# Gated delta rule stage: dense tiles in another order, a pair's two heads half a step apart, own query norms per chain

## The chip, the cores and the metric

One core of a Trainium2 chip. The metric is the device time of one execution in microseconds (us); the core is alone, so its time is the kernel's time. TensorE's clock has two levels here, 1.2 and 2.4 GHz; the profile gives the granted clock as a share of the upper one (PEclk, 1.00 = always 2.4 GHz, 0.5 = always 1.2 GHz).

## The reference, cut to what matters

A decoder trunk over 512 positions and 1024 channels in float32: attention, a feed-forward layer, a gated delta rule layer (the stage that changes), a second feed-forward layer. The stage that changes computes:

```python
def gated_deltanet(u, w_in, conv_w, a_log, dt_bias, norm_gain, w_out):
    proj = u @ w_in                                   # 1024 -> q 1024, k 1024, v 2048, z 2048, b 16, a 16
    qkv = silu(causal_dwconv(proj[..., :QKV], conv_w))    # 4 taps over positions
    q = repeat(l2_norm(q) * 128 ** -0.5, 2)           # 8 q/k heads serve 16 v heads
    k = repeat(l2_norm(k), 2)
    o = chunk_gated_delta_rule(q, k, v, g(a), beta(b))
    o = rms_norm(o, norm_gain) * silu(z)
    return o.reshape(B, S, 2048) @ w_out

def step(state, inp):                                 # one chunk of positions, all heads
    v_new = u_c - w_c @ state
    o = qd_c @ state + qk_c @ v_new
    state = state * g_last + kd_c.T @ v_new
```

Inside a chunk u and w come from a unit lower-triangular system in k, beta and the decays.

## The kernel before

**Dense tiles.** Every projection is made of weight tiles of 128 x 1024. `weight` loads a tile (DMA issued by SyncE, `raw`, L136), ScalarE casts it to `whi` (L137), VectorE subtracts to get `wlo` (L138). `dense` then issues 24 matmuls of 128 x 512, three products (L148, L149, L150) for each of 8 k-steps, into one PSUM tile.

**The queue.** Everything that is not a dense tile is a generator. `pump` is called after every second k-step (6 dense matmuls, one unit of `now`) and runs the generators that are due; a generator yields the number of units until its next piece. So the program's order on each engine is written out when the program is built: pieces of generators stand between groups of dense matmuls, which cover their latencies on TensorE. Each engine works its list in order.

**The stage, about 594 to 1156 us of the profiled execution.** First the 8 k tiles. `post_qk` and `post_v` convolve a tile (`conv`: L563, three VectorE steps L565, L566), turn it by four TensorE transposes (`turn`, L573) and store it in DRAM (kt, vd). Then 23 to 24 tiles in the order "zzqzzqzzqzzqzzzzzzzzqqqq" (z: gates, stored as zd by L752; q: queries), then the 16 v tiles, then the output projection `gout` in 2 halves of 8 tiles each (a part of 6 k-steps, then the last 2 when their heads are done; the sum into the residual `hp` is L784).

Beside them run: decays of the 8 head pairs (TensorE L820 to L828, matrices D and kk); `solve`, which inverts the 32 x 32 diagonal blocks of all systems on VectorE in 30 steps of two instructions (L863 `tm<-X`, L865 `X<-X,tm`), yields after every second step, and stores the inverse X twice: as it is (Td, L869) and, through ScalarE copies L874, transposed (Nd, L875). `recur` then takes the 8 pairs one after the other. `prologue` of a pair loads kk, D, kt, qd, the blocks NT (L924) and TT (L928) and joins the blocks by small matmuls: L938, L949/L950, L961 (query times key), L969, L976, with VectorE's x (L942, L971), D (L963) and `qd` (L972, the queries times a decay row loaded from DRAM) between them and ScalarE's kd (L980). `chain` of a pair is the recurrence over 4 blocks of 128 positions, both heads in each step: L1001 (key times state S), L1003 (o), vb on VectorE (L1006), L1010 (solve times vb), vn on ScalarE (L1012), L1017 (state update), L1019 (o), squares of o (L1020), S (L1023 or L1027). `epilogue` makes the norm (`rsqrt`, L163 to L169), scales o (L1050), turns it, multiplies by the silu of z (L1054) and splits it for `gout`. The prologue of pair hk+1 is advanced step by step together with the chain of pair hk. All chains need `rq`, a norm over the squares of all 8 q tiles.

Of the kernel before, what the change touches and what calls it, by code (L numbers as in the profile page):

```python
# [17 lines left out]
P = 128  # L18
T = 512
NB = 4  # L20
# [6 lines left out]
def layout(x, positions, mixer_norm, ffn_norm, attn_w_in, attn_q_gain, attn_k_gain, attn_sinks,  # L27
# [29 lines left out]
    a["gout"] = c(gdn_w_out[0].reshape(2, 8, P, KT, P).transpose(0, 3, 2, 1, 4)).reshape(2, KT, P, 1024)  # L57
# [13 lines left out]
class Builder:  # L71
# [598 lines left out]
    def gdn(self, h, hd, stack, after):  # L670
# [13 lines left out]
        self.ssk = ss["k"]  # L684

        def post_qk(nm, j, ps):
# [14 lines left out]
            if j == 7 and nm == "q":  # L701
                self.rq = self.inv_norm(ss["q"], "rq")
                V.tensor_scalar(self.rq, self.rq, float(P ** -0.5), None, op0=ALU.mult)
                ready.add("rq")

        def post_v(hh, ps):
# [8 lines left out]
            self.aux.dma_start(d["v"][hh // 2, :, hh % 2], four(vb))  # L715
# [26 lines left out]
        count = {"z": 0, "q": 0}  # L742
        for nm in "zzqzzqzzqzzqzzzzzzzzqqqq":
            j = count[nm]
            count[nm] += 1
            if nm == "q":
                self.spawn(post_qk("q", j, self.in_tile(j, un)))
            else:
# [3 lines left out]
                self.aux.dma_start(d["z"][j // 2, :, j % 2], four(z))  # L752
            enter()
        for hh in range(16):
            self.spawn(post_v(hh, self.in_tile(16 + hh, un)))
            enter()
# [3 lines left out]
        for half in range(2):  # L760
            have = lambda n: lambda: all(("o", hh) in ready for hh in range(8 * half, 8 * half + n))
            early = 2
            self.until(have(6))
            part = []
            for m in range(KT):
                if half == 0:
                    nc.sync.dma_start(hp[m], hd[m])
                hi, lo = self.weight(self.ins["gout"][half, m])
                ps = self.psum()
                for k in range(6):  # L770
                    s = slice(k * P, (k + 1) * P)
                    self.mm3(ps, (hi[:, s], lo[:, s]), outs[8 * half + k], k == 0, False)
                    if k % 2:
                        self.pump()
                part.append((m, ps, hi, lo))
                if m < early - 1:
                    continue
                self.until(have(8))
                for m, ps, hi, lo in part:
                    for k in (6, 7):  # L780
                        s = slice(k * P, (k + 1) * P)
                        self.mm3(ps, (hi[:, s], lo[:, s]), outs[8 * half + k], False, k == 7)
                    self.pump()
                    V.tensor_tensor(hp[m], hp[m], ps, op=ALU.add)  # L784
                    if half == 1:
                        after(m, hp[m])
                part = []
# [3 lines left out]
    def decays(self, sp, X, ready):  # L791
# [24 lines left out]
        for hk in range(8):  # L816
# [14 lines left out]
            self.aux.dma_start(d["D"][hk], D)  # L831
# [10 lines left out]
            yield 2  # L842
        ready.add("systems")

    def solve(self, sp, X, ready):
# [14 lines left out]
        for j in range(1, 31):  # L860
# [5 lines left out]
            if j % 2 == 0:  # L866
                yield 1
        nc.gpsimd.memset(X.rearrange("p i s c -> p i (s c)")[:, :, ::33], 1.0)
        self.aux.dma_start(d["T"].rearrange("m p i s c -> (m p) i s c"), X)  # L869
        for i in range(2):  # L870
            for b in range(2):
# [3 lines left out]
                self.aux.dma_start(d["N"].rearrange("m p i c s -> (m p) i c s")[:, i, cs], nat)  # L875
        ready.add("solved")

    def recur(self, rx, ready, outs):
        nxt = self.prologue(rx, 0, ready)
        w = yield from nxt  # L880
        for hk in range(8):
            cur = w
            chain = self.chain(rx, hk, cur, ready)
# [236 lines left out]
```

## Time and profile before

| | |
|---|---|
| time, median of 3 runs | 1555.14 us (1555.0 to 1555.92) |
| time of the profiled execution | 1552.91 us |
| its span | 1551.0 us |
| PE busy in the span | 1488.9 us, 96% |
| DVE / ACT / POOL busy | 890.0 / 686.7 / 10.4 us |
| mean granted clock | 0.982 |
| chains: first and last start of L1010 | 857.7 and 1109.9 us |

The span is what the trace shows; 1.9 us of the profiled execution lie outside of it, and it was 2.2 us shorter than the median run. PE is TensorE, PEld its weight load, DVE VectorE, ACT ScalarE, POOL GpSimd, SPq SyncE's instructions that issue DMAs. An engine's idle time is put down to what released it.

### The profile page before, as it was taken

The page shows a single profiled execution, that of the slowest core. Times are in us where ns is not written, and L with a number is a line of the kernel's source. Part 1 is how long each engine was busy: PE and PEld are TensorE (multiplying, and loading weights), DVE is VectorE, ACT ScalarE, POOL GpSimd, SP SyncE. Part 2 cuts the span into 40 slices and gives each one's busy share as a digit, 9 for nine tenths or more (in the row PEclk, how much of TensorE's full clock was granted, in tenths as well). Part 3 has the DMA queues.
Part 4 walks back from the last instruction along what each step waited for, and adds up shares of the span by engine and source line. Part 5 has one row for each costly group of instructions (what it writes and reads, how often), then busy time and mean ns, then how long its engine had stood idle before and what let it go on. Part 6 is the DMA issues. An engine that isn't in the chain of part 4 may idle for free.

```text
span 1551.0 us, 21045 instructions
## 1 busy us (share of the span) xinstructions
PE 1488.9 (96%) x7962; PEld 1228.9 (79%) x7962; DVE 890.0 (57%) x1759; ACT 686.7 (44%) x1576; POOL 10.4 (1%) x21
## 2 busy tenths in 40 slices
PE   7998999999999999999969998999999999999998
PEld 7965788888888888788748777878788888888887
DVE  7575765446535557754846356655566535544652
ACT  6687643223313345665335455644543323332331
POOL 0000000000000000000000000000000000000000
PEclk9998999999999999999979998999999999999999
DMA  5201233223333233367663444453132333222232
GB/s 179 69 25 32 82 109 95 96 95 95 98 100 102 96 129 119 122 203 244 203 212 113 126 150 147 156 144 109 57 108 95 98 102 99 95 95 96 95 103 74
DMA packets 83084, 177.09 MB, mean 114 GB/s; under 512 B 31272, under 2 KB 35368, under 8 KB 82728
## 3 DMA queue, kind: packets, MB, share of 16 engines
q1 hardware_dynamic: 82984, 175.76, 35.7%
q8 instruction: 62, 1.02, 0.3%
q14 instruction: 38, 0.31, 0.1%
HBM read 149.42 MB, written 26.31 MB: 113 GB/s over the span
## 4 chain that ended last, share of the span: by engine, by line
PE 85%; DVE 5%; DMA 5%; ACT 4%; issue 1%; SPq 0%; POOL 0%; DVEq 0%
PE ps L148 25%; PE ps L149 25%; PE ps L150 25%; DMA qd<-rowd 3%; ACT sc L520 1%; PE ps L573 1%; DVE wlo L138 1%; PE ps L545 1%; PE ps L961 1%; PE ps L1010 1%; DVE sc L514 1%; PE ps L1017 1%; PE ps L1003 1%; PE ps L1019 1%; PE ps L511 1%
## 5 line engine op out<-in xcount | busy, mean ns | idle before, releaser
L148 PE MATMUL ps<-a,whi 128*128 128x512 f32 x1736 | 691.1, 398 | 3.5 <-ACT whi L137 2.3
L149 PE MATMUL ps<-a,whi 128*128 128x512 f32 x1736 | 680.4, 392 | 0.0
L150 PE MATMUL ps<-a,wlo 128*128 128x512 f32 x1736 | 680.0, 392 | 0.1
L137 ACT CAST whi<-raw 128x1024 fp32r<-128x1024 f32 (+1 forms) x239 | 242.5, 1015 | 474.1 <-PE ps L149 406.3
L148 PEld LDWEIGHTS ps<-a,whi 128*128 128x128 f32 x1736 | 327.2, 189 | 76.6 <-ACT a L143 3.4
L150 PEld LDWEIGHTS ps<-a,wlo 128*128 128x128 f32 x1736 | 327.1, 188 | 70.3 <-DVE wlo L138 0.3
L149 PEld LDWEIGHTS ps<-a,whi 128*128 128x128 f32 x1736 | 327.4, 189 | 65.8 <-DVE a L144 1.1
L138 DVE TENSOR_TENSOR wlo<-raw,whi 128x1024 fp32r<-128x1024 f32 (+1 forms) x239 | 280.7, 1175 | 96.5 <-ACT whi L137 94.1
L258 DVE TENSOR_TENSOR h<-h,ps 128x512 f32<-128x512 f32 x48 | 33.0, 688 | 148.5 <-PE ps L150 148.5
L243 DVE TENSOR_TENSOR t<-ps,rbc 128x512 f32<-128x512 f32 x48 | 33.2, 691 | 106.6 <-PE ps L150 106.4
L249 DVE TENSOR_TENSOR t<-ps,rbc 128x512 f32<-128x512 f32 x48 | 33.2, 692 | 90.8 <-PE ps L150 90.8
L247 ACT ACTIVATE t<-t 128x512 f32<-128x512 f32 x48 | 30.4, 632 | 97.4 <-DVE t L246 97.4
L148 PE MATMUL ps<-whi,a 128*128 128x256 f32 x192 | 57.3, 299 | 9.1 <-ACT a L192 9.1
L149 PE MATMUL ps<-wlo,a 128*128 128x256 f32 x192 | 55.6, 290 | 0.5 <-DVE wlo L138 0.5
L150 PE MATMUL ps<-whi,a 128*128 128x256 f32 x192 | 55.6, 290 | 0.0
L148 PEld LDWEIGHTS ps<-whi,a 128*128 128x128 f32 x192 | 38.0, 198 | 11.2 <-ACT a L192 9.1
L143 ACT CAST a<-t 128x512 fp32r<-128x512 f32 x48 | 30.0, 624 | 33.0 <-DVE t L250 33.0
L244 ACT ACTIVATE t<-t,cols 128x512 f32<-128x512 f32 x48 | 38.9, 811 | 2.0 <-DVE t L243 2.0
L565 DVE SCALAR_TENSOR_TENSOR t<-ps,cols,t 128x511 f32<-128x511 f32 (+2 forms) x48 | 35.8, 746 | 6.5 <-ACT t L563 6.0
L149 PEld LDWEIGHTS ps<-wlo,a 128*128 128x128 f32 x192 | 38.2, 199 | 0.7 <-DVE wlo L138 0.7
L150 PEld LDWEIGHTS ps<-whi,a 128*128 128x128 f32 x192 | 38.0, 198 | 0.1
L246 DVE SCALAR_TENSOR_TENSOR t<-t,cols,t 128x510 f32<-128x510 f32 x48 | 36.0, 750 | 1.7
(255 smaller groups left out, 1410.3 us busy)
## 6 DMA issues: line engine op xcount, KB each, us to landing
raw<-in_up SPq DMA_DIRECT2D x96, 512.0 KB, 3.7
raw<-in_down SPq DMA_DIRECT2D x48, 512.0 KB, 3.6
raw<-in_gin SPq DMA_DIRECT2D x48, 512.0 KB, 3.8
raw<-in_gout SPq DMA_DIRECT2D x16, 512.0 KB, 3.9
raw<-in_win SPq DMA_DIRECT2D x10, 512.0 KB, 3.9
raw<-in_wout SPq DMA_DIRECT2D x16, 256.0 KB, 2.6
zd<-t SPq DMA_DIRECT2D x16, 256.0 KB, 3.2
Dd<-D SPq DMA_DIRECT2D x8, 512.0 KB, 2.7
```

Of the source, the lines that this page charges most:

```text
L137: nc.scalar.copy(hi[:, s], raw[:, s])
L138: nc.vector.tensor_tensor(lo[:, s], raw[:, s], hi[:, s].bitcast(F32), op=ALU.subtract)
L148: mm(ps, w[0], x[0], start=first, stop=False)
L149: mm(ps, w[0], x[1], start=False, stop=False)
L150: mm(ps, w[1], x[0], start=False, stop=last)
L243: nc.vector.tensor_tensor(g, gu[0], self.bc, op=ALU.mult)
L244: nc.scalar.activation(y, g, AF.Identity, bias=self.col(C_FB + l * 24 + j), scale=self.col(cw + 2))
L246: nc.vector.scalar_tensor_tensor(y[:, 2:], g[:, :T - 2], self.col(cw), y[:, 2:], op0=ALU.mult, op1=ALU.add)
L247: nc.scalar.activation(y, y, AF.Silu)
L249: nc.vector.tensor_tensor(t, gu[1], self.bc, op=ALU.mult)
L258: nc.vector.tensor_tensor(h[m], h[m], ps, op=ALU.add)
L565: nc.vector.scalar_tensor_tensor(dst[:, i:], g[:, :T - i], self.col(cw + 3 - i), dst[:, i:], op0=ALU.mult, op1=ALU.add)
```

## The change

1. **Order.** After the k tiles: "zzqzzvzzvzzqzzvzzvzzzz", more tiles while `solve` runs, then "qvv" six times, each tile when the chains come to need it (`r < 3 * started`), between parts of `gout`, whose weights are laid out in 4 quarters of 4 tiles; a quarter runs when its four heads are done. A counter `live` bounds the buffers held.
2. **Grain.** The stage's tiles pump after every k-step, by half a unit (3 dense matmuls).
3. **Chains.** The two heads of a pair stand half a step apart, each with its own instructions (L1001's one 128 x 256 matmul becomes two of 128 x 128). The query norm `rq` is gone: the scale of q drops out of the final norm except in its EPS term, which `ep` now carries per head, so a chain needs its own pair's q tile only. `recur` starts the next pair's prologue as a process of its own.
4. **Prologue.** kd and qd are loaded first and multiplied on GpSimd (two ops each), NT and TT next, D and vb last; shorter yields; `solve` yields after every step.
5. **Stores** of kt, v, z, D and Nd are issued by ScalarE's queue, not SyncE's.
6. **Epilogue.** Squares as two 128 x 512 ACT ops and two DVE reductions per pair, in place of eight ACT ops with accumulation; one of the two heads is scaled on DVE.

```diff
-    def pump(self):
-        self.now += 1
+    def pump(self, w=1):
+        self.now += w
...
             if k % grain == grain - 1:
-                self.pump()
+                self.pump(grain / 2)
...
-        self.dense(ps, hi, lo, u)
+        self.dense(ps, hi, lo, u, grain=1)
...
-                self.aux.dma_start(d["kt"][j], t)
+                nc.scalar.dma_start(d["kt"][j], t)
...
-            if j == 7 and nm == "q":
-                self.rq = self.inv_norm(ss["q"], "rq")
...
-        for nm in "zzqzzqzzqzzqzzzzzzzzqqqq":
+        for nm in "zzqzzvzzvzzqzzvzzvzzzz":
+            tile_in(nm)
         self.until(lambda: "solved" in ready)
...
+        rest, r, g = "qvv" * 6, 0, 0
+        while r < len(rest) or g < 12:
+            q = g // 4
+            if r < len(rest) and (r < 3 * self.started or not have(4 * q + 4)):
+                tile_in(rest[r])
...
+            elif have(4 * q + 4):
...
+                W = self.weight(self.ins["gout"][q, g % 4])
+                for m in (g % 4 * 2, g % 4 * 2 + 1):
+                    ps = self.psum()
+                    part(ps, m, W, q, range(4))
+                    end(ps, m, q)
...
+        self.until(lambda: have(14))
+        begun = []
+        for m in range(4):
...
+            part(ps, m, W, 3, (0, 1))
+            begun.append((ps, W))
+        self.until(lambda: have(16))
...
-            self.aux.dma_start(d["D"][hk], D)
+            nc.scalar.dma_start(d["D"][hk], D)
...
-            if j % 2 == 0:
-                yield 1
+            yield 1
...
-                self.aux.dma_start(d["N"].rearrange("m p i c s -> (m p) i c s")[:, i, cs], nat)
+                nc.scalar.dma_start(d["N"].rearrange("m p i c s -> (m p) i c s")[:, i, cs], nat)
...
+        self.aux.dma_start(qd, self.rowd[1, 1:, hs].partition_broadcast(P))
+        for j in range(2):
+            self.aux.dma_start(kd[:, j], d["kt"][hk].rearrange("p (n c) -> p n c", n=NB)[:, :NB - 1])
         self.aux.dma_start(kk, d["kk"][:, hs])
-        self.aux.dma_start(D, d["D"][hk])
-        self.aux.dma_start(kt, d["kt"][hk].rearrange("p (n c) -> p n c", n=NB))
-        self.aux.dma_start(qd, self.rowd[1, 1:, hs].partition_broadcast(P))
...
-            yield 16
+            yield 4
...
-        yield 3
+        self.aux.dma_start(D, d["D"][hk])
+        if early:
+            self.aux.dma_start(vb, d["v"][hk])
+        yield 4 if hk else 8
+        for j in range(2):
+            ck = self.ck[:, :NB - 1, 2 * hk + j].unsqueeze(2).broadcast_to([P, NB - 1, P])
+            nc.gpsimd.tensor_tensor(kd[:, j], kd[:, j], ck, op=ALU.mult)
...
+        for j in range(2):
+            nc.gpsimd.tensor_tensor(qd[:, :, j], self.qT[hk][:, P:].rearrange("p (n c) -> p n c", c=P), qd[:, :, j], op=ALU.mult)
...
-        V.tensor_tensor(qd, self.qT[hk][:, P:].rearrange("p (n c) -> p n c", c=P).unsqueeze(2).broadcast_to([P, 3, 2, P]), qd, op=ALU.mult)
...
-                nc.tensor.matmul(pk[:, :2 * P], self.kT[hk][:, s], S.rearrange("p j c -> p (j c)"), start=True, stop=True)
...
+                    mm(pk[:, col(j)], self.kT[hk][:, s], S[:, j], start=True, stop=True)
+                    V.scalar_tensor_tensor(vb[:, j, n], pk[:, col(j)], at(self.ca, j), vb[:, j, n], op0=ALU.mult, op1=ALU.add)
+                    mm(o[j][:, s], qd[:, n - 1, j], S[:, j], start=True, stop=False)
+                    yield 1 if j else 0.5
...
+                mm(pv[:, col(j)], TT[:, j, n], vb[:, j, n], start=True, stop=True)
+                nc.scalar.copy(vn[:, j], pv[:, col(j)])
+                yield 0.5
...
+            nc.scalar.activation(ob[j], o[j], AF.Square)
+            V.tensor_reduce(mo[:, j], four(ob[j]), axis=AX.X, op=ALU.add)
```

SyncE's list at the end of the solve (X the inverse, Nd and Td its stores in DRAM, NT and TT their loads, zd the store of a z tile, raw a weight tile), before:

```order
L136 DMA raw<-in_gin 128x1024 x4
L875 DMA Nd<-t_6710 128x512
L869 DMA Td<-X 128x2048
L875 DMA Nd<-t_6713 128x512
L875 DMA Nd<-t_6716 128x512
L875 DMA Nd<-t_6719 128x512
L752 DMA zd<-t_6722 128x512
L752 DMA zd<-t_6756 128x512
L752 DMA zd<-t_6790 128x512
L752 DMA zd<-t_6824 128x512
L752 DMA zd<-t_6858 128x512
L924 DMA NT<-Nd 32x8x32 x3
```

The same place on SyncE after the change:

```order
L1063 DMA z<-zd 128x1024
L136 DMA raw<-in_gin 128x1024 x6
L898 DMA Td<-X 128x2048
L950 DMA NT<-Nd 32x8x32 x2
L954 DMA TT<-Td 32x8x32 x2
L950 DMA NT<-Nd 32x8x32
L954 DMA TT<-Td 32x8x32 x6
L958 DMA vb<-vd 128x1024
L136 DMA raw<-in_gin 128x1024
```

The stores of Nd and zd have left the list (ScalarE issues them now), and two TT loads stand between the NT loads.

VectorE's list inside the solve (each step is a pair L863, L865), before:

```order
L863 TENSOR_TENSOR tm<-X 128x468
L865 TENSOR_TENSOR X<-X,tm 128x2x13x18
L863 TENSOR_TENSOR tm<-X 128x476
L972 TENSOR_TENSOR qd<-a_6120,qd 128x768
L865 TENSOR_TENSOR X<-X,tm 128x2x14x17
L138 TENSOR_TENSOR wlo<-raw,whi 128x1024
```

The same place on VectorE after the change (L893 and L895 are the steps, t_6675 a v tile in its convolution):

```order
L138 TENSOR_TENSOR wlo<-raw,whi 128x1024
L895 TENSOR_TENSOR X<-X,tm 128x2x11x20
L565 SCALAR_TENSOR_TENSOR t_6675<-ps,cols,t_6675 128x511
L893 TENSOR_TENSOR tm<-X 128x456
L565 SCALAR_TENSOR_TENSOR t_6675<-ps,cols,t_6675 128x510
L895 TENSOR_TENSOR X<-X,tm 128x2x12x19
L565 SCALAR_TENSOR_TENSOR t_6675<-ps,cols,t_6675 128x509
L893 TENSOR_TENSOR tm<-X 128x468
L138 TENSOR_TENSOR wlo<-raw,whi 128x1024
```

`qd` no longer stands between two steps; convolutions of v tiles do, since v tiles are now made during the solve.

TensorE's list inside a chain step (L148 to L150 are dense matmuls of a tile), before:

```order
L1010 MATMUL ps<-vb,TT 128x128 x2
L148 MATMUL ps<-a_5192,whi 128x512
L149 MATMUL ps<-a_5193,whi 128x512
L150 MATMUL ps<-a_5192,wlo 128x512
L148 MATMUL ps<-a_5237,whi 128x512
L149 MATMUL ps<-a_5238,whi 128x512
L150 MATMUL ps<-a_5237,wlo 128x512
L1017 MATMUL ps<-vn,kd 128x128 x2
L1019 MATMUL ps<-vn,D 128x128 x2
```

The same step on TensorE after the change (L1043, L1049 and L1054 are the new numbers of L1010, L1017 and L1019):

```order
L1043 MATMUL ps<-vb,TT 128x128
L148 MATMUL ps<-a_9705,whi 128x512
L149 MATMUL ps<-a_9706,whi 128x512
L150 MATMUL ps<-a_9705,wlo 128x512
L1049 MATMUL ps<-vn,kd 128x128
L1054 MATMUL ps<-vn,D 128x128
L148 MATMUL ps<-a_9283,whi 128x512
L149 MATMUL ps<-a_9284,whi 128x512
L150 MATMUL ps<-a_9283,wlo 128x512
L1049 MATMUL ps<-vn,kd 128x128
L1054 MATMUL ps<-vn,D 128x128
```

The pair of each matmul is parted by three dense matmuls, the first head's L1043 standing three more ahead of this piece.

## Rows read from the trace of the kernel before

**Rows 1.** Stretches of the span: busy us of each engine, PEclk, DMA share, GB/s.

```profile
860.00:940.00 80.00, 72.24 (x632) 61.91 (x632) 44.00 (x106) 40.77 (x127) 2.52 (x4) 0.88 0.44 128
920.00:940.00 20.00, 14.85 (x147) 12.67 (x146) 11.42 (x33) 9.16 (x30) 0.96 (x1) 0.84 0.48 151
940.00:1000.00 60.00, 57.37 (x463) 49.13 (x463) 35.27 (x75) 34.17 (x101) 2.53 (x4) 0.97 0.48 146
1000.00:1060.00 60.00, 55.56 (x472) 47.44 (x471) 35.77 (x90) 31.95 (x101) 2.53 (x4) 1.00 0.51 154
1060.00:1090.00 30.00, 27.70 (x239) 23.37 (x238) 17.19 (x43) 13.04 (x39) 0.00 (x0) 0.94 0.34 102
1160.00:1551.00 391.00, 387.05 (x1711) 320.24 (x1710) 197.04 (x237) 120.46 (x142) 0.00 (x0) 1.00 0.29 95
```

**Rows 2.** TensorE's waits, 594 to 1160 us: in total, times, longest.

```profile
PE ps L938 <- DMA NT<-Nd: 14.4, 1, 14.4
PE ps L949 <- DVE nt L167: 5.1, 1, 5.1
PE ps L949 <- DVE x L942: 3.7, 4, 2.5
PE ps L1017 <- ACT vn L1012: 3.6, 3, 2.6
PE ps L949 <- issue: 3.2, 2, 2.2
PE ps L1010 <- DMA vb<-vd: 2.5, 1, 2.5
PE ps L148 <- ACT whi L137: 2.3, 1, 2.3
PE ps L573 <- ACT t L1050: 1.2, 1, 1.2
```

**Rows 3.** VectorE's waits, 640 to 1121 us.

```profile
DVE qd L972 <- DMA qd<-rowd: 28.6, 7, 6.9
```

**Rows 4.** SyncE's waits, 640 to 1121 us.

```profile
SPq L752 <- ACT t L751: 17.4, 10, 7.2
```

**Rows 5.** TensorE in time: start, us, instruction, idle before it and its releaser.

```profile
721.96 0.40 PE L828 MATMUL ps<-a,selr 128*128 128x512 f32 x1
...
795.03 0.31 PE L938 MATMUL ps<-NT,kk 32*32 32x32 f32 x2 [14.43 <-DMA NT<-Nd]
```

**Rows 6.** VectorE in time, start and end of the solve and one step.

```profile
736.71 2.35 DVE L858 TENSOR_TENSOR X<-X,bk 128x1024 f32<-128x1024 f32 x2
...
761.87 0.96 DVE L972 TENSOR_TENSOR qd<-a,qd 128x768 f32<-128x768 f32 x1 [2.37 <-DMA qd<-rowd]
...
784.77 0.26 DVE L865 TENSOR_TENSOR X<-X,tm 128x60 f32<-128x60 f32 x1
```

**Rows 7.** ScalarE in time, behind the solve.

```profile
785.30 3.00 ACT L874 COPY t<-X 128x512 f32<-128x512 f32 x3
```

**Rows 8.** SyncE in time, behind the solve.

```profile
786.40 2.27 SPq L875 DMA_DIRECT2D Nd<-t  x3
788.81 3.30 SPq L752 DMA_DIRECT2D zd<-t  x5
792.16 1.90 SPq L924 DMA_DIRECT2D NT<-Nd  x3
```

**Rows 9.** Groups, 594 to 1160 us: busy, mean ns, idle before and releasers.

```profile
L138 DVE TENSOR_TENSOR wlo<-raw,whi 128x1024 fp32r<-128x1024 f32 x64 | 78.3, 1223 | 63.6 <-ACT whi L137 61.2 <-PE ps L1017 2.3
...
L565 DVE SCALAR_TENSOR_TENSOR t<-ps,cols,t 128x511 f32<-128x511 f32 x16 | 12.0, 748 | 6.1 <-ACT t L563 6.0
...
L784 DVE TENSOR_TENSOR h<-h,ps 128x512 f32<-128x512 f32 x16 | 10.9, 684 | 14.3 <-PE ps L150 14.3
...
L911 POOL MEMSET TT<- 128x1024 f32 x8 | 7.7, 959 | 818.7 <-DMA Dd<-D 718.4 <-PE ps L1010 61.8 <-ACT z L1045 15.4
L972 DVE TENSOR_TENSOR qd<-a,qd 128x768 f32<-128x768 f32 x8 | 7.7, 958 | 28.6 <-DMA qd<-rowd 28.6
```

More of the change, by code (lines that the diff above doesn't have):

```diff
@@ L751, in gdn @@
                 nc.scalar.copy(z, ps)
-                self.aux.dma_start(d["z"][j // 2, :, j % 2], four(z))
+                nc.scalar.dma_start(d["z"][j // 2, :, j % 2], four(z))
             enter()
-        for hh in range(16):
-            self.spawn(post_v(hh, self.in_tile(16 + hh, un)))
-            enter()
+        for nm in "zzqzzvzzvzzqzzvzzvzzzz":
+            tile_in(nm)
         self.until(lambda: "solved" in ready)
@@ L759, in gdn @@
         hp = self.load_h(stack)
[L760 to L768, printed above, removed]
-                ps = self.psum()
[L770 to L787, printed above, removed]
@@ new lines, in gdn, with part, end @@
+        have = lambda n: all(("o", hh) in ready for hh in range(n))
+        def part(ps, m, W, q, ks):
+            hi, lo = W
+            for k in ks:
+                s = slice((m % 2 * 4 + k) * P, (m % 2 * 4 + k + 1) * P)
+                self.mm3(ps, (hi[:, s], lo[:, s]), outs[4 * q + k], k == 0, k == 3)
+                self.pump(0.5)
+        def end(ps, m, q):
+            V.tensor_tensor(hp[m], hp[m], ps, op=ALU.add)
+            if q == 3:
+                after(m, hp[m])
+        rest, r, g = "qvv" * 6, 0, 0
@@ new lines, in gdn @@
+        self.until(lambda: have(14))
+        begun = []
+        for m in range(4):
+            if m % 2 == 0:
+                W = self.weight(self.ins["gout"][3, m // 2])
+            ps = self.psum()
+            part(ps, m, W, 3, (0, 1))
+            begun.append((ps, W))
+        self.until(lambda: have(16))
+        for m in range(KT):
+            if m < 4:
+                ps, W = begun[m]
+                part(ps, m, W, 3, (2, 3))
+            else:
+                if m % 2 == 0:
+                    W = self.weight(self.ins["gout"][3, m // 2])
+                ps = self.psum()
+                part(ps, m, W, 3, range(4))
+            end(ps, m, 3)
@@ L977, in prologue @@
         nc.scalar.copy(TT[0:64, :, :, 64:128], view(pt[0:64, :], 64))
-        for j in range(2):
-            for n in range(3):
-                nc.scalar.activation(kd[:, j, n], kt[:, n], AF.Copy, scale=self.ck[:, n, 2 * hk + j:2 * hk + j + 1])
-        yield 1
-        while ("v", 2 * hk) not in ready or ("v", 2 * hk + 1) not in ready:
+        if not early:
+            while not have_v():
+                yield 0.5
+            self.aux.dma_start(vb, d["v"][hk])
+            yield 3
+        else:
@@ L983, in prologue, with chain @@
             yield 1
-        self.aux.dma_start(vb, d["v"][hk])
-        yield 2
-        return TT, D, vb, kd, qd
-    def chain(self, rx, hk, tiles, ready):
+        return TT, D, vb, kd, qd, mo
+    def chain(self, rx, hk, tiles):
         nc = self.nc
         V = nc.vector
-        TT, qk, vb, kd, qd = tiles
+        mm = nc.tensor.matmul
+        TT, qk, vb, kd, qd, mo = tiles
         S = rx.tile([P, 2, P], F32, tag="S", name="S", bufs=2)
         o = [self.psum() for _ in range(2)]
-        self.o = o
-        self.mo = self.small.tile([P, 2, NB], F32, tag="mo", name="mo")
-        self.ob = [self.t2() for _ in range(2)]
+        col = lambda j: slice(j * P, (j + 1) * P)
@@ L1021, in chain @@
-            if n < NB - 1:
-                if n == 0:
-                    nc.scalar.copy(S, pu[:, :2 * P].rearrange("p (j c) -> p j c", j=2))
-                else:
-                    for j in range(2):
-                        h = 2 * hk + j
-                        V.scalar_tensor_tensor(S[:, j], S[:, j], self.egl[:, n, h:h + 1], pu[:, j * P:(j + 1) * P], op0=ALU.mult, op1=ALU.add)
-            if n < NB - 1:
-                yield
-    def epilogue(self, rx, hk, tiles, ready, outs):
+                mm(pv[:, col(j)], TT[:, j, n], vb[:, j, n], start=True, stop=True)
@@ L1051, in epilogue @@
+        for n in range(NB):
+            s = slice(n * P, (n + 1) * P)
+            nc.scalar.activation(ob[1][:, s], o[1][:, s], AF.Copy, scale=rs[:, 1, n:n + 1])
         yield 2
+        while self.live + 4 > 36:
+            yield 0.5
+        self.live += 4
         for j in range(2):
```

131 lines of the change are left out of this document (69 added, 62 removed).

## The prediction

> **What bounds the kernel now.** I read the page first: TensorE is busy 96% of the span, so only its idle time and its clock can be won. In the second feed-forward layer, which the change leaves alone, 1711 matmuls take 387.05 us at a clock of 1.00 [rows 1], 0.226 us each; that is the price of a dense matmul below, and the rate that the stage lacks. The stretches then show where it is lost inside the changed stage: from 860 to 940 us TensorE works 72.24 of 80 us at a clock of 0.88, then 57.37 of 60 at 0.97, and 27.70 of 30 at 0.94 [rows 1]. The waits of TensorE, of the stage alone, name the culprits: one of 14.4 us for the NT blocks, 5.1, 3.7 and 3.2 us at L949 in a prologue, 3.6 for vn, 2.5 for vb, 2.3 for a weight cast, 1.2 at the last epilogue [rows 2]. Two rows on other engines explain some of these. VectorE stands in its list seven times, 28.6 us in all and up to 6.9 at once, at `qd` L972 for a load [rows 3]; whatever is behind it, `x` and the norm's steps L167 among it, comes late, and these are what L949 waits for. SyncE stands 17.4 us in ten waits at the stores of z tiles [rows 4], with weight loads behind it.
>
> **The NT wait, 14.4 us.** Two paths race. TensorE: the last decay matmul starts at 721.96, the first matmul on NT at 795.03 after 14.43 us idle [rows 5], so TensorE arrives at 780.6. Between them I count 240 dense matmuls in the order (54.3 us), the 2.3 us weight wait and two turns with small things in the 1.8 us that are left, 0.9 a turn. In the changed order 283 dense matmuls and four turns stand there: 64.0 + 3.6, no weight wait (below), so TensorE arrives at 722.2 + 67.6 = 789.8. The solve: it starts behind L858, at 736.71 + 2.35 = 739.06, and its last step ends at 785.03 [rows 6], 46.0 us. Two `qd` steps leave it, one with a wait of 2.37 + 0.96 [rows 6] and one of 0.96, 4.3 us; seven convolution steps of v tiles come in at 0.748 [rows 9], 5.2 us. It ends at 786.0. Behind it the copies took to 788.30 [rows 7], and NT's matmul came 6.7 us later. Of these, 0.5 was the wait behind the z stores of 3.30 us for five [rows 8], which leave. New on the path: ScalarE issues the Nd stores itself between its copies, 1.4 (two of them at 0.66, the price of a store on SyncE [rows 8]); a z copy of 0.6 in place of a 1.0 cast; two TT loads between the NT loads, 1.3 (1.90 us for three such loads [rows 8]). NT is there at 786.0 + 3.3 + 6.7 - 0.5 + 1.4 - 0.4 + 1.3 = 797.8, the wait is 8.0 us: a gain of **6.4**. The ends are no wait and 17 (rivals).
>
> **Weight wait, 2.3 us.** The cast's tile came late because its load was issued behind a z store that waited for its copy. With the stores gone from SyncE no load stands behind one: **+2.3**. The Trainium skill, page "DMA: Bandwidth & Descriptors", section "Issuing engines are not separate DMA queues", speaks against it: transfers from several engines end on the same DMA engines, and spreading the issue saves only issuing time. By that the 2.3 would stay and the sum be that much smaller. The row of SyncE's waits [rows 4] shows something else than issuing time, a queue that stands for another engine's result, which the page doesn't treat; I keep the gain.
>
> **Prologue waits, 5.1 + 3.7 + 3.2 = 12.0 us.** `qd` leaves VectorE for GpSimd, which waits for the load alone, and the load is issued first instead of fourth. Nothing else on VectorE waits for a load in the prologue. Late next would be GpSimd's own kd and qd: four ops per pair of 128 x 384. No row shows such an op; a memset of 128 x 1024 takes 0.959 there [rows 9], so 0.36 by elements and, with three streams in place of one, 1.1 as the upper bound; VectorE's `qd` gives 0.48 (0.958 for 768 [rows 9]). Four cost 1.4 to 4.4 us in a pair's 32 us (chains run some 255 us for eight pairs), and their first reader is the chain behind the prologue: no cost. I take **+12.0**; the lower end is that half stays, since the waits at L949 are also the sequence of small steps itself.
>
> **vb, 2.5 us.** v tiles are made before they are asked for in pairs 0 to 3 and by need after; vb is loaded when both are stored, with three units between load and use (18 dense matmuls, 4.1 us). **+2.5**, none at the lower end.
>
> **Hops in the chains, 3.6 us.** Before, six dense matmuls (1.36 us) stood between a step's matmul and its reader. Now three, the other head's matmul, and three more; but a copy or a product is for one head, half as wide. The three waits came of ScalarE being late, and it now issues some fifty stores as well, at up to 0.66 each [rows 8], but loses 48 scalings for kd and 48 squares. I take 2.2 left: **+1.4**, ends 0 and 3.6. More instructions on TensorE (48 of 128 x 256 become 96 of 128 x 128) cost the same columns; I take 0.
>
> **Other work.** VectorE gains sixteen more sums at 0.684 [rows 9], sixteen reductions priced alike (nearest row of 512 columns) and eight half scalings: some 28 us, less 7.7 for `qd`. It is busy 44 of 80 us in the chains' busiest stretch [rows 1], so this lies in gaps: nothing, if the waits above stay away; each late step on it that reaches a chain is what the second rival prices.
>
> **Tail.** In the last epilogue a square and two reductions of 512 columns stand in a row ahead of the norm, three times 0.68, where before only the last block's square did. The 1.2 us wait [rows 2] becomes 2.7: **-1.5**. Ends: none and three times this.
>
> **Clock.** From 860 to 1090 the share missing from full clock is 80 x 0.12 + 60 x 0.03 + 30 x 0.06 = 13.2 us; at 92% busy 12 us of work lost [rows 1]. The stretches below full clock are those with the waits in them. Without them I leave 2.5 (the prologue of the first pairs): **+9.5**; half of it at the lower end. The clock lost around the NT wait I leave as it is.
>
> **Sum.** 6.4 + 2.3 + 12.0 + 2.5 + 1.4 - 1.5 + 9.5 = 32.6. On the profiled execution, 1552.9: 1520.3. That run was 2.2 below the median, so 1522.5, **1522**.
>
> **Rivals.**
> *The NT wait goes altogether.* For it: arrival and data differ by 8.0 only, and each is a long sum; a shorter hop through DRAM, or more dense matmuls than the turns leave room for, would do. Another 8.0 and 2.5 of clock: 1512. Chance 0.13.
> *Waits in the chains only halve.* The prologue stays a series of small steps between TensorE, VectorE and ScalarE, its yields are shorter than before, and VectorE has 20 us more to do. Half of 12.0 + 2.5 stays, 7.2, and 3.5 of the clock: 1533. Chance 0.19.
> *GpSimd holds up VectorE.* Eight of its new ops stand in the order during the solve, ahead of the memset that the Nd copies wait for. If each stops VectorE for its 1.1 us, the solve ends 8.8 later, and the NT wait is 16.8: 1531. Nothing in the trace shows it either way, GpSimd is busy 2.5 of 80 us there [rows 1]. Chance 0.08. The Trainium skill, "GPSIMD Engine Reference", section "Engine selection", puts two-input elementwise work at about half VectorE's speed on GpSimd; by it an op would be an estimated 0.96, near my upper bound.
> *The stores' move does nothing*, and a wait like the 2.3 remains: 1525. Chance 0.06.
> *The other side: the clock.* Half-sized pieces make small matmuls of 128 x 128 a finer mix with dense ones over all the chains. The 255 us of chains lose 0.92 x 255 = 235 us times what is missing from full clock. Without the 23.1 us of idle time that the sum wins and the 12 that the clock costs now, the change breaks even at 35.1 / 235, a mean clock of 0.85 there. The worst stretch so far, 920 to 940, has 0.84 [rows 1]; were the clock down half of the time over all the chains, 0.75, 58.7 us are lost: 1555.1 - 35.1 + 58.7 = 1579. Against it: 1000 to 1060 holds 1.00 with the same kinds of matmuls [rows 1]. Chance 0.05.
> *Nothing comes of it* (one new wait of 30 us takes the place of these, such as a tile that comes late because the order by need holds it): 1555. Chance 0.04.
>
> **How the numbers follow.** The forecast has 0.45; two runs of this kernel differ by about 0.1%, so I call under 0.2% (3 us) no change. All cases but the last two are faster: 0.91; same 0.03; slower 0.06. The range takes the first rival with 4 us of its own, and reaches up to the second with 7: 1508 to 1540, with the two last cases and the ends of the others left out.
>
> **What would show it.** Right: VectorE has no wait for `qd`; SyncE none at the z stores; TensorE's wait for NT is between 5 and 10 us; L981, the place of L949, under 3 us in all; the clock from 860 to 1090 at 0.97 or more; the stage ends some 33 us earlier and the feed-forward layer behind it takes as long as before. Wrong: a wait of TensorE for GpSimd's kd or qd, for a weight tile, or a clock under 0.9 in the chains; the solve longer than 48 us.

## The result, and the profile after

The changed kernel takes 1512.22 us (median of 4 runs, 1511.24 to 1513.94), the kernel before in the same comparison 1555.07; the ratio is 0.974 with a 95% interval of 0.9717 to 0.9764. The forecast was 1522 in 1508 to 1540: right in direction and range, 10 us too high. The two profiled executions are 39.0 us apart (1552.91 and 1513.94), and the sum of the prediction, 32.6, is to be held against these; that leaves 6.4 us. The other 3.9 lie in which executions were profiled: 2.2 us below the median before, 1.7 above it after.

The head of the page of the changed kernel: TensorE is busy 9.9 us less, and idle 29 us less.

```profile
span 1512.1 us, 21017 instructions
PE 1479.0 (98%) x8010; PEld 1218.7 (81%) x8010; DVE 907.3 (60%) x1761; ACT 661.6 (44%) x1424; POOL 41.4 (3%) x53
```

TensorE's waits in the stage of the changed kernel (columns as in [rows 2]); L970, L1043 and L1036 are the new numbers of L938, L1010 and L1001, and L210 belongs to the norm behind the stage:

```profile
PE ps L970 <- DMA NT<-Nd: 5.7, 1, 5.7
PE ps L210 <- DVE rc L169: 3.9, 1, 3.9
PE ps L1043 <- ACT vn L1044: 1.9, 2, 1.1
PE ps L573 <- ACT t L566: 1.2, 1, 1.2
PE ps L1036 <- DVE vb L1037: 0.8, 2, 0.6
PE ps L573 <- DVE t L1076: 0.7, 1, 0.7
```

TensorE waits for nothing in the prologues behind NT any more: all that L949 stood for in [rows 2] is gone. The largest wait is still NT, at 5.7 in place of 14.4. One wait is new, 3.9 us at L210. Stretches of the changed kernel, to be held against [rows 1]:

```profile
787.00:800.00 13.00, 7.34 (x50) 4.83 (x49) 0.85 (x2) 6.91 (x12) 0.00 (x0) 0.74 0.95 293
860.00:940.00 80.00, 79.19 (x663) 67.06 (x662) 57.13 (x118) 40.21 (x108) 9.92 (x13) 1.00 0.52 149
1113.00:1124.00 11.00, 7.06 (x30) 5.82 (x29) 6.42 (x20) 2.44 (x3) 0.00 (x0) 0.69 0.41 133
1124.00:1512.00 388.00, 384.55 (x1697) 318.08 (x1695) 194.38 (x234) 118.34 (x139) 0.00 (x0) 1.00 0.29 94
```

In the chains TensorE works 79.19 of 80 us at a clock of 1.00, where it worked 72.24 at 0.88. Inside the stage and at the norm behind it the clock is down only around the two long waits that are left, NT (0.74) and L210 (0.69). The feed-forward layer behind runs as before.

### The profile page after: what moved, and what is told of

Its sections match the earlier page's. It is cut to its first block, busy times and chain, and to the rows that moved or that the text cites. A ratio compares the mean times of both kernels' runs of the same rounds, so it can differ in the third digit from the quotient of the medians.

```text
span 1512.1 us, 21017 instructions
## 1 busy us (share of the span) xinstructions
PE 1479.0 (98%) x8010; PEld 1218.7 (81%) x8010; DVE 907.3 (60%) x1761; ACT 661.6 (44%) x1424; POOL 41.4 (3%) x53
## 3 DMA queue, kind: packets, MB, share of 16 engines
q8 instruction: 63, 1.03, 0.3%
## 5 line engine op out<-in xcount | busy, mean ns | idle before, releaser
L148 PE MATMUL ps<-a,whi 128*128 128x512 f32 x1736 | 696.2, 401 | 0.7 <-ACT a L143 0.7
L150 PE MATMUL ps<-a,wlo 128*128 128x512 f32 x1736 | 679.1, 391 | 0.0
L148 PEld LDWEIGHTS ps<-a,whi 128*128 128x128 f32 x1736 | 326.7, 188 | 68.9 <-ACT a L143 3.6
L150 PEld LDWEIGHTS ps<-a,wlo 128*128 128x128 f32 x1736 | 326.0, 188 | 68.8
L148 PE MATMUL ps<-whi,a 128*128 128x256 f32 x192 | 57.2, 299 | 8.3 <-ACT a L192 8.3
L150 PE MATMUL ps<-whi,a 128*128 128x256 f32 x192 | 55.6, 290 | 0.0
L148 PEld LDWEIGHTS ps<-whi,a 128*128 128x128 f32 x192 | 38.0, 198 | 10.3 <-ACT a L192 8.3
L150 PEld LDWEIGHTS ps<-whi,a 128*128 128x128 f32 x192 | 37.9, 198 | 0.1
L565 DVE SCALAR_TENSOR_TENSOR t<-ps,cols,t 128x511 f32<-128x511 f32 (+2 forms) x48 | 35.6, 742 | 3.5 <-ACT t L563 3.3
```

Of the source, the lines that this page charges most:

```text
L148: mm(ps, w[0], x[0], start=first, stop=False)
L150: mm(ps, w[1], x[0], start=False, stop=last)
L565: nc.vector.scalar_tensor_tensor(dst[:, i:], g[:, :T - i], self.col(cw + 3 - i), dst[:, i:], op0=ALU.mult, op1=ALU.add)
```

## The experiments

Each ratio is to the kernel before on the same chip (its time was 1547 to 1559 us over all of these runs). The changed kernel's own is 0.974, 0.9717 to 0.9764. Where a ratio and a difference of medians disagree, the ratio counts, since each is to runs of the kernel before made beside it.

| run | what differs | median us | ratio, 95% interval |
|---|---|---|---|
| before_qd_dve_first | before, qd load written first | 1551.31 | 1.0002, 0.9988 to 1.0015 |
| before_qd_pool | before, qd on GpSimd, load written first | 1527.29 | 0.985, 0.983 to 0.9871 |
| before_act_stores | before, stores on ScalarE | 1549.57 | 0.9992, 0.9977 to 1.0007 |
| after_qd_dve_late | after, qd on VectorE behind x2, load late | 1525.48 | 0.9837, 0.982 to 0.9853 |
| after_qd_dve | after, qd on VectorE, load early | 1528.83 | 0.9839, 0.9826 to 0.9853 |
| after_sync_stores | after, stores on SyncE | 1515.77 | 0.9755, 0.9741 to 0.9769 |
| after_cover | after, 4 units more ahead of NT | 1513.11 | 0.9734, 0.9714 to 0.9754 |
| after_norm_late | after, 2 units more ahead of L210 | 1506.81 | 0.9698, 0.9685 to 0.9711 |
| after_pair_same | after, both heads at one step | 1515.25 | 0.9771, 0.9758 to 0.9784 |
| before_qd_pool_cover | before_qd_pool, 7 units more ahead of NT | 1520.55 | 0.9799, 0.9776 to 0.9823 |
| norm_cover_pc | late norm, cover, heads together; steps not shorter, see below | 1512.24 | 0.9752, 0.9739 to 0.9766 |
| norm_cover_hs | late norm, cover, shorter steps, half step | 1502.55 | 0.9701, 0.9682 to 0.9721 |

**Where qd is multiplied: four runs.** The theory: VectorE's list stands at `qd` for its load, and what is behind it is late for L949. Rivals: a prologue is late of itself, or the load comes late wherever it is written. VectorE, then TensorE, in time in the kernel before, at the longest of these waits:

```profile
928.71 0.96 DVE L972 TENSOR_TENSOR qd<-a,qd 128x768 f32<-128x768 f32 x1 [6.87 <-DMA qd<-rowd]
...
934.49 0.43 DVE L942 TENSOR_TENSOR x<-ps,nbk 32x256 f32<-32x256 f32 x1
```

```profile
935.17 0.26 PE L949 MATMUL ps<-TT,x 32*32 32x32 f32 x2 [5.15 <-DVE nt L167]
```

L949 reads the `x` that is ready at 934.92. What `x` is made from, the result of L938, was there at 927.6, while VectorE stood at `qd`.

before_qd_dve_first (one line moved, the load written first):

```diff
+        self.aux.dma_start(qd, self.rowd[1, 1:, hs].partition_broadcast(P))
         self.aux.dma_start(kk, d["kk"][:, hs])
...
-        self.aux.dma_start(qd, self.rowd[1, 1:, hs].partition_broadcast(P))
```

> The kernel before, with one line moved: a pair's qd load is issued first of its prologue's loads in place of fourth; the multiplication stays on VectorE at its old place. Theory A (the waits at L949 come of VectorE standing for the qd load, 28.6 us in 7 waits): VectorE's wait at qd shrinks to under 15 us, TensorE's waits at L949 from 12.0 to under 6, the time falls by 4 to 14 us to about 1541 to 1551. Rival B (a prologue is late of itself, as a series of small steps): L949 keeps its 10 to 12 us, the time moves by less than 3 us. Rival C (the load is late because its buffer comes free late, wherever it stands in SyncE's list): VectorE's wait at qd stays above 20 us, the time moves by less than 3 us.

Nothing moved: the ratio is 1.0002. VectorE in this run stands at `qd` 32.7 us in eight waits, and TensorE at L949 as before. SyncE in time in this run (L916 loads kt, L913 is the moved qd load):

```profile
921.13 0.42 SPq L916 DMA_DIRECT2D kt<-ktd  x1
921.81 0.37 SPq L913 DMA_DIRECT2D qd<-rowd  x1
```

VectorE in time in the same run:

```profile
930.33 0.96 DVE L972 TENSOR_TENSOR qd<-a,qd 128x768 f32<-128x768 f32 x1 [6.15 <-DMA qd<-rowd]
```

The load still stands behind kt in SyncE's list, as it did in the kernel before: written first, it was not issued first, since its buffer comes free only with the last L1003 of two pairs ago. VectorE has the data 8.5 us after the issue. This is what the run's rival C expected. So the run doesn't show what an early load would do; it shows that the place in the source does not make it early.

before_qd_pool (the load as there, and the product on GpSimd):

```diff
-        V.tensor_tensor(qd, self.qT[hk][:, P:].rearrange("p (n c) -> p n c", c=P).unsqueeze(2).broadcast_to([P, 3, 2, P]), qd, op=ALU.mult)
+        for j in range(2):
+            nc.gpsimd.tensor_tensor(qd[:, :, j], self.qT[hk][:, P:].rearrange("p (n c) -> p n c", c=P), qd[:, :, j], op=ALU.mult)
```

> The kernel before with qd multiplied on GpSimd (two ops of 128 x 384 per pair) and its load issued first. Theory A: no wait of VectorE for qd is left, L949 waits under 3 us in place of 12.0, the clock from 860 to 1090 rises to 0.96 or more; the time falls by 12 to 21 us to about 1534 to 1543. Rival B (series of small steps): L949 keeps 8 us or more, the time falls by less than 6 us. Rival C (GpSimd takes over the wait): TensorE waits for qd at L1003 instead, 5 us or more, the time falls by less than 6 us.

The ratio is 0.985, some 23 us, more than half of the whole change by one operation on another engine, and more than the 12 to 21 us expected. TensorE's waits in the stage in this run, its three longest:

```profile
PE ps L938 <- DMA NT<-Nd: 11.8, 1, 11.8
PE ps L949 <- DMA TT<-Td: 3.5, 4, 1.8
PE ps L1011 <- DMA vb<-vd: 2.8, 1, 2.8
```

One stretch of the same run:

```profile
860.00:940.00 80.00, 78.69 (x657) 67.49 (x656) 51.83 (x118) 47.81 (x148) 6.82 (x9) 1.00 0.54 155
```

TensorE's idle pieces over 0.3 us sum to 25.9 in place of 39.9, and the clock of this stretch is 1.00 in place of 0.88. The span is 25.5 us shorter: 14 us of these waits and, as in the prediction's count, 10 to 11 of clock. Of the waits 2.6 us are at NT, where the solve is 2.1 us shorter without its two `qd` steps. L949 still waits some 5 us in all, mainly for the loads of TT, where under 3 was expected. GpSimd's own wait:

```profile
POOL qd L973 <- DMA qd<-rowd: 49.9, 7, 13.4
```

GpSimd stands for the load longer than VectorE did, 49.9 us, and TensorE doesn't wait for it: its waits name neither L1004, the reader, nor GpSimd. The wait was moved to a list with nothing urgent behind it. That contradicts rival B (L949 keeps 8 us or more) and this run's rival C (TensorE waits for `qd` at its reader instead). What the runs don't separate is the product itself, 0.96 us each time, from the wait ahead of it, since both leave VectorE together; but it is the smaller part, 7.7 us in eight [rows 9] against 28.6 of waits, and a wait like the 5.15 us above is longer than it.

after_qd_dve_late (the reverse, in the changed kernel: load behind kd and kk, product behind x2, as before) and after_qd_dve (load early as in the change, one VectorE op at GpSimd's place):

```diff
-        for j in range(2):
-            nc.gpsimd.tensor_tensor(qd[:, :, j], self.qT[hk][:, P:].rearrange("p (n c) -> p n c", c=P), qd[:, :, j], op=ALU.mult)
+        V.tensor_tensor(qd, self.qT[hk][:, P:].rearrange("p (n c) -> p n c", c=P).unsqueeze(2).broadcast_to([P, NB - 1, 2, P]), qd, op=ALU.mult)
```

> The changed kernel with qd multiplied on VectorE behind x2 as before, and its load issued behind kd and kk. Theory A: VectorE stands at qd again, 10 to 30 us in all, TensorE's waits in the prologues come back with 6 to 12 us, the clock there falls; the time rises by 8 to 21 us to about 1520 to 1533. Rival B (the shorter, earlier prologue is what removed the waits): TensorE's waits in the prologues stay under 2 us, the time rises by less than 3 us.

> The changed kernel with qd multiplied on VectorE by one op of 128 x 768, at the same place of the program and with the load first as it is. Theory A (VectorE's list stands for the load wherever the op comes before its load has landed; GpSimd stood 37.0 us for qd in six waits): VectorE stands at qd for 10 to 35 us, TensorE's waits rise by 5 to 12 us, the time rises by 8 to 20 us to 1520 to 1532. Rival B (with the early load the data are there): no wait at qd, the time within 3 us. Rival C (GpSimd's ops slow VectorE's: a step of the solve took 0.96 us in place of 0.65 while one ran): the solve gets shorter by 1 to 2 us and the time falls by 1 to 4 us.

The ratios rise from 0.974 to 0.9837 and 0.9839: 15 us each, with all else of the change in place. VectorE in after_qd_dve:

```profile
DVE qd L990 <- DMA qd<-rowd: 24.8, 5, 6.4
DVE qd L990 <- PE ps L1042: 6.3, 1, 6.3
```

VectorE stands again, although the load is written first. TensorE's idle pieces are 23.3 us in place of 14.0 (22.2 in after_qd_dve_late), but none is at L981, where theory A of after_qd_dve_late expected 6 to 12 us: other lines of the chains and turns wait longer than before. The time came as expected, the place didn't. That these lines wait for what stood behind `qd` is the reading that fits both directions; it wasn't followed line by line.

**The stores: two runs.** before_act_stores:

```diff
-            self.aux.dma_start(d["D"][hk], D)
+            nc.scalar.dma_start(d["D"][hk], D)
```

and so for kt, v, z and Nd.

> The kernel before with the stores of kt, v, z, D and Nd issued by ScalarE's queue, nothing else. Theory A (SyncE's list stands for results of other engines at these stores): the weight wait of 2.3 us goes, the NT wait falls from 14.4 to 11 to 13 us, the time falls by 3 to 7 us to about 1548 to 1552. Rival B, the Trainium skill's rule that spreading the issue saves only issuing time: within 1.5 us of before.

The ratio is 0.9992 and its interval holds 1. TensorE's waits in this run, the first two:

```profile
PE ps L938 <- DMA NT<-Nd: 17.2, 1, 17.2
PE ps L949 <- DVE x L942: 8.9, 5, 5.5
```

The weight wait of 2.3 us is gone, and SyncE stands at no z store; but TensorE comes to NT that much earlier and waits 17.2 us there in place of 14.4. A gain ahead of a wait for something else is given back at that wait. The time of this run agrees with the rule of the Trainium skill, page "DMA: Bandwidth & Descriptors", section "Issuing engines are not separate DMA queues", that issuing from another engine saves only issuing time.

after_sync_stores puts them back:

```diff
-                nc.scalar.dma_start(d["z"][j // 2, :, j % 2], four(z))
+                self.aux.dma_start(d["z"][j // 2, :, j % 2], four(z))
```

> The changed kernel with the stores of kt, v, z, D and Nd back on SyncE. Changed kernel: 1512.2 us. Theory A (the place of the stores matters here, since the wait for NT is now the largest one left and Nd's stores would queue on SyncE behind weight loads that stand for wlo): the NT wait rises from 5.7 to 8 to 11 us, a weight wait of 1 to 3 us is back, the time rises by 3 to 8 us to 1515 to 1520. Rival B (as in the kernel before, where the stores' move alone gave 0.9992 with an interval that holds 1: a wait gone at one place is stood at another): within 2 us.

SyncE's longest wait for these stores in it, then TensorE's:

```profile
SPq L711 <- ACT t L710: 33.1, 8, 6.8
```

```profile
PE ps L970 <- DMA NT<-Nd: 5.2, 1, 5.2
...
PE ps L148 <- DVE tm L893: 1.6, 1, 1.6
PE ps L150 <- DVE wlo L138: 1.6, 1, 1.6
```

A weight is late again (3.2 us), the NT wait is not longer (theory A was wrong there). Both sides of it came later: the solve took 52.6 us from its first step to its last in place of 48.1, and TensorE reached NT 5.1 us later behind the last decay matmul. The interval overlaps that of the changed kernel: 3.6 us by the medians, 2.3 by the ratios, not settled.

**The cover at NT: two runs.** after_cover and before_qd_pool_cover:

```diff
-        yield 4 if hk else 8
+        yield 4 if hk else 12
```

```diff
-            yield 16
+            yield 23
```

> The changed kernel with four units more between the first pair's loads of NT and its first matmul (a yield of 12 in place of 8; 306 dense matmuls in place of 283 between the last decay matmul and the first on NT). Theory A (dense work covers the NT wait and the chains have dense work to spare): the wait of 5.7 us falls under 1, the clock behind it stays at 1.00, the time falls by 5 to 8 us to 1504 to 1507. Rival B (the 23 dense matmuls are missing from the chains' end, where they cover steps): as much wait comes back in the last two pairs, the time moves by less than 2 us.

> The kernel before with qd on GpSimd and its load first (1527.3 us, NT wait 11.8) and 7 units more of dense work ahead of the first pair's matmuls (a yield of 23 in place of 16; 288 dense matmuls in place of 240 since the last decay matmul). Theory A (more cover hides the NT wait whatever the order of tiles): the NT wait falls under 3 us, the time to 1515 to 1519, nearly that of the changed kernel. Rival B (as with the cover added to the changed kernel: the dense matmuls are missing behind, and the wait comes back at the chains' end or at the output projection's first half): within 3 us of 1527.

In the changed kernel the wait at NT falls to 0.8 us, and the time stays, where theory A had 1504 to 1507. TensorE's longest waits in after_cover:

```profile
PE ps L573 <- DVE t L1076: 4.7, 1, 4.7
PE ps L210 <- DVE rc L169: 3.5, 1, 3.5
```

The 23 dense matmuls were missing at the last pair's epilogue, 4.7 us in place of 0.7: its rival B. In before_qd_pool, where the v tiles were still in stock, the same cover does pay: the wait at L938 falls from 11.8 to 3.0 and the ratio from 0.985 to 0.9799, somewhat less than expected (1515 to 1519 us). So the smaller NT wait does not need the new order of tiles, only dense work that isn't missed later. From here to the changed kernel's 0.974 some 9 us are left; the order of the tiles, the grain, the query norms and the epilogue were not tried alone, so how they share these stays open.

**The new wait at L210: one run.** after_norm_late lets the norm's second group of matmuls come 12 dense matmuls later in the feed-forward layer behind the stage:

```diff
         self.rsqrt(r, v, NB)
-        yield 2
+        yield 4 if self.first is None else 2
```

(`first` is None behind the gated delta rule stage alone.)

> The changed kernel with two units more (12 dense matmuls of the feed-forward layer) between the norm's two groups of matmuls L202 and L210 behind the stage. Theory A (L210 waits 3.9 us for VectorE's rsqrt, since 2 dense matmuls stand ahead of it in place of 12 before, and the clock is at its lower level for some 5 us behind): wait and low clock go, the time falls by 4 to 7 us to 1505 to 1508. Rival B (VectorE is what is late, with 25.1 of 28 us busy there, and its next steps hold TensorE at the next tile): the time falls by less than 2 us.

The ratio is 0.9698, below the changed kernel's without overlap. TensorE in time in the changed kernel, then VectorE between L202 and L210:

```profile
1113.37 0.95 PE L202 MATMUL ps<-ones,t 128*128 128x1 f32 x8
...
1118.84 2.08 PE L210 MATMUL ps<-ident,rc 128*128 128x128 f32 x8 [3.94 <-DVE rc L169]
```

```profile
1114.44 1.22 DVE L138 TENSOR_TENSOR wlo<-raw,whi 128x1024 fp32r<-128x1024 f32 x1
...
1115.91 1.22 DVE L138 TENSOR_TENSOR wlo<-raw,whi 128x1024 fp32r<-128x1024 f32 x1
```

Two things make this wait. Only 2 dense matmuls stand between L202 and L210, where 11 stood before; and these two `wlo` products stand between the steps of the norm on VectorE, where none stood before, so that from L204 to the last step 4.4 us pass in place of 2.4. The nine missing matmuls (2.0 us at 0.23 each) and the 2.0 us of delay together are the 3.9 us of the wait.

The same place in after_norm_late:

```profile
1111.69 0.95 PE L202 MATMUL ps<-ones,t 128*128 128x1 f32 x8
...
1117.57 1.16 PE L210 MATMUL ps<-ident,rc 128*128 128x128 f32 x8
```

The stretch 1113 to 1124 in after_norm_late:

```profile
1113.00:1124.00 11.00, 10.98 (x52) 8.89 (x52) 7.78 (x19) 3.82 (x5) 0.00 (x0) 1.00 0.36 115
```

L210 comes as long behind L202 as it did (5.9 us, 5.5 in the changed kernel), now with 21 dense matmuls between; wait and low clock (0.69 in the changed kernel) are both gone.

**The half step: three runs.** after_pair_same yields only behind the second head (the same dense matmuls between a step and its reader):

```diff
                     mm(o[j][:, s], qd[:, n - 1, j], S[:, j], start=True, stop=False)
-                    yield 1 if j else 0.5
+                yield 1.5
...
                 nc.scalar.copy(vn[:, j], pv[:, col(j)])
-                yield 0.5
+            yield 1
...
                 mm(o[j][:, s], qk[:, j, n], vn[:, j], start=n == 0, stop=True)
-                yield 1 if j else 0.5
+            yield 1.5
```

> The changed kernel with the two heads of a pair at the same step of the chain again (per-head instructions kept, the same number of dense matmuls between a step and its reader: 9, 6 and 9). Theory A (the cover, not the half step, is what counts): within 3 us of the changed kernel's 1512.2, TensorE's waits in the chains within 2 us of its 4 us. Rival B (the half step is needed, since both heads' small ops come at once on VectorE and ScalarE): waits in the chains rise by 4 us or more, the time by 4 to 10 us.

0.9771 is slower than the changed kernel by 3 us by the medians and by 5 by the ratios, between theory A and rival B. Its waits are not longer (12.6 us of idle pieces, 14.0 in the changed kernel), which contradicts rival B's reason; TensorE is busy 2.0 us longer, and why stays open. The last two runs join the late norm, the cover of after_cover, and steps that were meant to have 21 dense matmuls in place of 24. norm_cover_pc has the heads together (yields 1.25, 1, 1.25), norm_cover_hs keeps the half step (the last yield of a step 0.5 for both heads).

> The changed kernel with the late norm (1506.8 us alone), the cover of four units at NT (whose wait came back in the last pair's epilogue, 4.7 us, when it was added alone), and chains with both heads at one step and 21 dense matmuls in place of 24 per step, so that the chains end some 90 dense matmuls earlier. Theory A (the end of the chains is what the cover took from): neither the NT wait nor the wait in the last epilogue stands, the time falls to 1499 to 1503. Rival B (shorter steps bring back waits for vn and vb in the chains): these rise by 4 us or more and the time stays at 1505 or above.

> As the run before it, but with the half step kept and 21 dense matmuls per step (the last yield of a step 0.5 in place of 1). Theory A: 1499 to 1503, within 2 us of the run before it. Rival B (waits for vn and vb come back): 1505 or above. Between the two runs the half step decides if they differ by more than 3 us.

TensorE's first waits in norm_cover_pc, then in norm_cover_hs:

```profile
PE ps L573 <- DVE t L1076: 4.4, 1, 4.4
PE ps L1036 <- DVE vb L1037: 3.4, 2, 1.7
```

```profile
PE ps L1036 <- DVE vb L1037: 3.4, 3, 1.8
PE ps L573 <- ACT t L566: 1.2, 1, 1.2
PE ps L970 <- DMA NT<-Nd: 1.0, 2, 0.8
```

These two runs do not show what the half step is worth, since norm_cover_pc did not get its shorter steps. The stage's tiles pump by half a unit, so a piece that yields 1.25 comes after 1.5. In the traces 684 dense matmuls stand between the first L1043 and the last L1054 of norm_cover_pc, as many as in after_pair_same, and 627 in norm_cover_hs. So the two differ in the length of a step as well. What they show is the other thing: with the half step and long steps (after_cover) the last epilogue waits 4.7 us, with both heads together and long steps (norm_cover_pc) 4.4, and with the half step and shorter steps (norm_cover_hs), whose last L1054 comes at 1072 us in place of 1088 in norm_cover_pc, that wait is gone. norm_cover_pc missed its 1499 to 1503 us; norm_cover_hs met them, though not the expected 2 us between the two.

Of the 9.0 us between their spans, 4.1 are idle pieces (10.5 and 6.4 us). TensorE is also busy 5.5 us less (1479.5 and 1474.0 us); what is in that stays open, apart from the clock behind the 4.4 us wait. norm_cover_hs has the lowest median, 1502.55, but its interval is that of after_norm_late: the two aren't told apart, and every run of either is below every run of the changed kernel.

## Why the prediction was right, point by point

| term | forecast us | measured us (two profiled executions) |
|---|---|---|
| NT wait | 6.4 | 8.8 (14.4 to 5.7) |
| weight wait | 2.3 | 2.3 (none left) |
| prologue waits at L949 | 12.0 | 12.0 (none left) |
| vb | 2.5 | 2.5 (none left) |
| vn | 1.4 | 1.7 (3.6 to 1.9) |
| tail | -1.5 | -3.4 (1.2 to 0.7 + 3.9) |
| clock, 860 to 1090 | 9.5 | 12 (none missing) |
| not in the sum | | 2 (small waits), -2 (clock behind L210) |
| sum | 32.6 | 36, of 39.0 |

So the 6.4 us that the sum lacks are NT (2.4), the clock (2.5), small waits (2) and the 3 us left, less what the wait at L210 and the clock behind it cost beyond the tail's 1.5 (4). About 1 of the 3 us left lies ahead of the stage (it begins 1 us earlier); 2 are not assigned.

**Prologue waits and clock: right, and the core of it.** The place (VectorE standing at `qd`) and the size held: both directions of the experiment give 15 to 23 us, 12 to 14 of waits in the kernel before and the clock that goes with them. One half of the reason fell: the load, written first, was not issued earlier in before_qd_dve_first, and in after_qd_dve VectorE stood for it all the same. The doubt behind the second rival, a series of small steps that keeps half of the waits, did not hold: in before_qd_pool some 5 us are left at L949, 3.5 of them for TT's loads.

**NT: right in place, with two errors that partly cancel.** TensorE arrived 68.1 us behind the last decay matmul, forecast 67.8. The solve took 48.7 us, forecast 46.9; from its end to the first NT matmul went 8.2 us, forecast 11.8. Rows of the changed kernel, VectorE, ScalarE's queue and SyncE in time:

```profile
785.07 0.27 DVE L895 TENSOR_TENSOR X<-X,tm 128x60 f32<-128x60 f32 x1
```

```profile
789.32 0.33 ACTq L904 DMA_DIRECT2D Nd<-t  x1
```

```profile
791.04 0.85 SPq L950 DMA_DIRECT2D NT<-Nd  x2
791.99 0.93 SPq L954 DMA_DIRECT2D TT<-Td  x2
793.02 0.42 SPq L950 DMA_DIRECT2D NT<-Nd  x1
```

The loads follow the last Nd store by 1.4 us; before, 3.5 lay between, nearly all of it the z stores of [rows 8], of which I counted 0.5. The two TT loads, counted with 1.3, cost nothing: the third NT load was issued 0.5 us before the matmul at 793.50, too late to be what it waited for (no NT load landed in under 2.0 us). The terms for the z stores (0.5, where the gap fell by 2.1) and for the TT loads (1.3) were mis-sized. The weight wait is bound to this one: before_act_stores shows that ahead of a longer NT wait its 2.3 us are worth nothing alone, so what I kept against the Trainium skill's rule can be a gain only together with a shorter NT wait. That it is one here is argued; after_sync_stores does not settle it.

**GpSimd holds up VectorE: a real effect, half the size of its rival.** The last section has the rows; the solve's 60 instructions took 34.0 us in all in place of 30.2, not 8.8 more. In after_qd_dve, where half of GpSimd's products are back on VectorE, they take 31.1. The solve came to 48.7 us, so one sign of being wrong did come, "the solve longer than 48 us": the NT term had left the effect out.

**Tail: wrong; that its sign came out right is luck.** I priced the last epilogue, 2.7 us, and it waits 0.7. What came in its place is the wait at the norm behind the stage, with two `wlo` products between its steps and 2 dense matmuls to cover it. VectorE is full there: with twice the sums into `hp`, and only 12 dense matmuls for each, it is busy 25.1 of the 28 us to 1113. "Nothing, if the waits stay away" was the step of mine that failed: VectorE's 28 us more were free in the chains and not in the last 28 us. The program asks for the same 2 units between L202 and L210 in both kernels; that 10 of these 12 dense matmuls came to stand ahead of L202 because the sums come late on VectorE is argued, not shown.

**The clock rival did not come:** 1.00 from 800 to 1113.

## What to carry to other kernels

Ask of each instruction that waits for a load what stands behind it on its engine: 28.6 us of waiting on VectorE cost some 23 us of time, and 49.9 on GpSimd left no wait on TensorE. Work moved ahead as cover has to be missed by nobody later; look at where the stock of it runs out. When an engine gets more to do, price it in the stretch where that engine is fullest, which here was the end of the stage.

## What the runs showed of the hardware

GpSimd's products slow VectorE's while they run, those that read two inputs from SBUF. The solve in the changed kernel, VectorE and GpSimd in time:

```profile
756.29 0.73 DVE L565 SCALAR_TENSOR_TENSOR t<-ps,cols,t 128x509 f32<-128x509 f32 x1
756.95 0.80 DVE L893 TENSOR_TENSOR tm<-X 128x468 f32<-128x468 f32 x1
757.67 1.85 DVE L138 TENSOR_TENSOR wlo<-raw,whi 128x1024 fp32r<-128x1024 f32 x1
759.44 1.27 DVE L895 TENSOR_TENSOR X<-X,tm 128x468 f32<-128x468 f32 x1
760.75 0.66 DVE L893 TENSOR_TENSOR tm<-X 128x476 f32<-128x476 f32 x1
```

```profile
754.87 2.38 POOL L991 TENSOR_TENSOR qd<-a,qd 128x384 f32<-128x384 f32 x2 [12.77 <-DMA qd<-rowd]
757.21 3.01 POOL L962 TENSOR_TENSOR kd<-kd,ck 128x384 f32<-128x384 f32 x2
```

Until 760.2 a wlo takes 1.85 us (1.223 in [rows 9]) and a step 1.27 where a larger one takes 0.66 right after; L565, which reads one of its inputs from PSUM, keeps its 0.73. At the start of the solve it is starker: under GpSimd's first products a step of 60 elements takes 1.03 us, 0.22 in the kernel before. The Trainium skill says so on its page "SBUF — State Buffer", section "Who interferes with whom": a VectorE instruction with two inputs in SBUF contends with a GpSimd instruction that reads SBUF, and one with a single SBUF input, outside the modes that use both ports, does not; this trace agrees. GpSimd's ops of 128 x 384 took 1.07 us (qd) and 0.92 (kd) on average, near the 0.96 that the prediction estimated.

The load of qd, one row repeated over the partitions, is slow for its size. DMA issues of the kernel before, with the median time to landing last:

```profile
raw<-in_gin SPq DMA_DIRECT2D x48, 512.0 KB, 3.8
...
qd<-rowd SPq DMA_DIRECT2D x8, 384.0 KB, 8.3
```

Why it takes 8.3 us was not tried.
